# Softmax with a relative position bias: first chunk in one load, bias table spread on chip from 16 packets, first store held until the fourth load has landed

## The chip, the cores and the metric

The kernel runs on one core of one Trainium2 chip. The metric is device time in microseconds (us); the time before is the median of three runs. Besides the compute engines (TensorE is not used here), the core has 16 DMA engines, which carry every transfer between HBM (main memory) and SBUF (on-chip memory). A transfer over 128 partitions is divided among all 16.

## The reference

`logits` is 2 x 8 x 2112 x 2112 in float32, `rel_bias` is 8 x 33. A bias that depends only on the head and on the distance of row and column, clipped to 16, is added; then a softmax runs over the last axis.

```python
rel_clipped = np.clip(pos[:, None] - pos[None, :], -16, 16) + 16
bias = rel_bias[:, rel_clipped]
logits = logits + bias[None]
exp = np.exp(logits - logits.max(axis=-1, keepdims=True))
out = exp / exp.sum(axis=-1, keepdims=True)
```

285 MB are read and as many written.

## The kernel before

Each of the 128 partitions owns 264 consecutive rows of 2112 numbers; 8 partitions make one head. The rows are worked through in chunks of R = 6 rows per partition, 44 chunks in all, in four buffers X[0] to X[3] (NBUF = 4). A chunk is one transfer of 128 runs of 50688 bytes in, and one of the same size out.

Setup builds in PSUM a strip M with the bias of a partition's first row at every distance (L118 to L155 on VectorE). It begins with the bias table: ScalarE issues a load (L97) that puts the whole 8 x 33 table on each of the 128 partitions, VectorE multiplies it by a head mask (L131) and sums over the heads (L135), so that `rbS` holds the 33 numbers of the partition's own head. GpSimd supplies two index tiles for the masks.

The main loop runs over groups of four chunks (24 rows). VectorE copies a window of M to F (`strip`, L160), and then for each buffer b: `add(b)` waits for the load (`ld[b]`) and in six instructions (L166) adds the bias and takes each row's extreme; ScalarE's `exps(b)` (L175) does the exponentials and their sums; `scale(b)` on VectorE multiplies by the reciprocals (L187), and each row raises `scaled` by one.

SyncE (SP) issues all large transfers on one queue (q1 in the profile), in an order written out by hand. First come the loads of chunks 0 to 3: chunk 0 as six transfers of one row each (L88; the first five count on the semaphore `pre`, the sixth on `ld[0]`), chunks 1 to 3 as one transfer each (L78). VectorE waits for `pre` before its first `strip`. Then comes `store(0, 0)` as soon as chunk 0 is scaled, and a loop whose order is: store the next chunk (L82), wait until the store before it has landed (`st[b]`), load the chunk four further on into that buffer (L78).

```python
store(0, 0)
with nc.Fori(0, ROWS - 2 * STEP + 1, STEP, engines=[ENG.SP]) as j:
    for b in range(NBUF):
        store(j + (b + 1) * R, (b + 1) % NBUF)
        take(nc.sync, st[b], 16)
        load(j + (b + NBUF) * R, b)
```

`take` waits for a semaphore and lowers it again (L74). `store` first takes six counts of `scaled`. Each of the 16 DMA engines raises a transfer's semaphore by one when its share is done, so a wait for 16 is a wait for all of them.

Of the kernel before, what the change touches and what calls it, by code (L numbers as in the profile page):

```python
# [15 lines left out]
def kernel(  # L16
# [6 lines left out]
    nc = tc.nc  # L23
    P = 128
    B, H, S, S2 = logits.shape
    assert S == S2
    MR = 16
    W = 2 * MR + 1
    ROWS = B * H * S // P
    PB = S // ROWS  # L30
    assert ROWS * P == B * H * S and PB * ROWS == S and PB == H == 8
    R = 6
    NBUF = 4
# [9 lines left out]
    X = [io.tile([P, R * S], FP32, tag=f"X{b}", name=f"X{b}") for b in range(NBUF)]  # L43
    F = io.tile([P, FW], FP32, tag="F", name="F")
    rbS = io.tile([P, W], FP32, tag="rbS", name="rbS")
# [3 lines left out]
    ip = io.tile([P, 3, PB], I32, tag="ip", name="ip")  # L49
# [3 lines left out]
    def view(t, offset, dims):  # L53

        return bass.AP(tensor=t.tensor, offset=t.offset + offset, ap=[[list(t.ap[0])[0], P]] + dims)

    def rows(t, j, n):

        return bass.AP(tensor=t.tensor, offset=t.offset + j * S, ap=[[ROWS * S, P], [1, n * S]])

    with tc.tile_critical(no_gpsimd_drain=True):
        ld = [nc.alloc_semaphore(f"ld{b}") for b in range(NBUF)]
# [3 lines left out]
        scaled = nc.alloc_semaphore("scaled")  # L66
        inv = nc.alloc_semaphore("inv")
        rb = nc.alloc_semaphore("rb")
        pre = nc.alloc_semaphore("pre")
        idx = nc.alloc_semaphore("idx")  # L70
        dve = nc.alloc_semaphore("dve")

        def take(eng, sem, n):
            eng.wait_ge(sem, n).then_inc(sem, -n)  # L74


        def load(j, b):
            nc.sync.dma_start(out=X[b][:, :], in_=rows(logits, j, R)).then_inc(ld[b], 16)  # L78

        def store(j, b, s0=0, n=R):  # L80
            take(nc.sync, scaled, n)
            nc.sync.dma_start(  # L82
                out=rows(out, j + s0, n), in_=X[b][:, s0 * S : (s0 + n) * S]
            ).then_inc(st[b], 16)


        for r in range(R):
            nc.sync.dma_start(  # L88
                out=X[0][:, r * S : (r + 1) * S], in_=rows(logits, r, 1)
            ).then_inc(ld[0] if r == R - 1 else pre, 16)  # L90
        for n in range(1, NBUF):
            load(n * R, n)

        rbB = view(F, 0, [[1, H * W]])
        nc.scalar.dma_start(  # L97
            out=rbB,
            in_=bass.AP(tensor=rel_bias.tensor, offset=rel_bias.offset, ap=[[0, P], [1, H * W]]),
        ).then_inc(rb, 16)  # L100
        nc.gpsimd.iota(ip[:, 0], pattern=[[0, PB]], base=0, channel_multiplier=1).then_inc(idx, 1)
        nc.gpsimd.iota(ip[:, 2], pattern=[[1, PB]], base=0, channel_multiplier=0).then_inc(idx, 1)  # L102

        v = nc.vector
        done = [0]

        def then(ins):
            done[0] += 1
            ins.then_inc(dve, 1)

        def settle():
            v.wait_ge(dve, done[0])

        SC = H * W
        mask = [F[:, SC + i * PB : SC + (i + 1) * PB] for i in range(9)]
        dp, dh, eq, hm, gt, le, lt, ra, rz = mask
        v.wait_ge(idx, 2)
        then(v.tensor_scalar(out=ip[:, 1], in0=ip[:, 0], scalar1=3, scalar2=7,  # L118
                             op0=ALU.logical_shift_right, op1=ALU.bitwise_and))
# [7 lines left out]
        for m, op in ((eq, ALU.is_equal), (gt, ALU.is_gt), (le, ALU.is_le), (lt, ALU.is_lt)):  # L127
# [4 lines left out]
            out=view(F, 0, [[W, H], [1, W]]), in0=view(F, 0, [[W, H], [1, W]]),  # L132
            in1=view(F, SC + 3 * PB, [[1, H], [0, W]]), op=ALU.mult))
        settle()
        then(v.tensor_reduce(out=rbS[:, :], in_=view(F, 0, [[1, W], [W, H]]),  # L135
                             axis=mybir.AxisListType.X, op=ALU.add))
        settle()
        low, high = rbS[:, W - 1 : W], rbS[:, 0:1]
        then(v.tensor_scalar(out=ra, in0=gt, scalar1=low, scalar2=None, op0=ALU.mult))  # L139
        then(v.tensor_scalar(out=rz, in0=gt, scalar1=low, scalar2=None, op0=ALU.mult))  # L140
        then(v.tensor_tensor(  # L141
            out=view(F, 0, [[W, PB], [1, W]]), in0=view(F, SC + 2 * PB, [[1, PB], [0, W]]),
            in1=view(rbS, W - 1, [[0, PB], [-1, W]]), op=ALU.mult))
# [6 lines left out]
            out=view(M, U, [[ROWS, PB], [1, W]]), in0=view(F, 0, [[W, PB], [1, W]]),  # L150
            in1=view(F, SC + 8 * PB, [[1, PB], [0, W]]), op=ALU.add))
        then(v.tensor_copy(out=view(M, U + W, [[ROWS, PB], [1, ROWS - W]]),  # L152
                           in_=view(F, SC + 7 * PB, [[1, PB], [0, ROWS - W]])))
        then(v.tensor_copy(out=M[:, 0:U], in_=low.to_broadcast([P, U])))  # L154
# [32 lines left out]
                    v.tensor_scalar_mul(out=x, in0=x, scalar1=rec[:, r : r + 1]).then_inc(scaled, 1)  # L187

        v.sem_inc(dve, -done[0])
        take(v, pre, 16 * (R - 1))  # L190
        with nc.Fori(0, ROWS - STEP + 1, STEP, engines=[ENG.DVE]) as j:  # L191
            strip(j)
            take(v, dve, 1)
# [6 lines left out]

        store(0, 0)
        with nc.Fori(0, ROWS - 2 * STEP + 1, STEP, engines=[ENG.SP]) as j:
            for b in range(NBUF):
# [39 lines left out]
```

## Time and profile before

| What | Value |
|---|---|
| Median of 3 runs | 1331.93 us (1330.07 to 1332.26) |
| Span of the profiled execution | 1327.7 us (the page gives no other time of it) |
| VectorE (DVE) busy | 976.6 us, 74% |
| ScalarE (ACT) busy | 575.2 us, 43% |
| GpSimd (POOL) busy | 0.4 us |
| Moved by DMA | 571.11 MB, 430 GB/s over the span |

The span runs from the first to the last instruction of one execution. In the profile, a strip is the span or a window of it in 40 slices, each digit the busy share in tenths. A line of the timeline gives the start, the duration, the engine, the line of the code and the operation; "SPq" and "ACTq" are the sequencers that issue DMAs, and an issue's duration is not that of the transfer. The DMA view of a window counts the packets that start in it: a chunk's packets are of 50688 bytes, and the tiny ones are the semaphore updates at the end of each DMA engine's share. For a line that issues DMAs, another view gives the times from issue to landing.

### The profile page before, as it was taken

The numbers are of one execution on the slowest core, as the hardware profiler recorded it, in microseconds if no ns is written. First come the engines' busy times: TensorE is split into PE (matmuls) and PEld (weight loads), VectorE is DVE, ScalarE is ACT, GpSimd is POOL, SyncE is SP. The second block draws the span as 40 slices with busy tenths as digits, with TensorE's granted clock in tenths as the row PEclk, the third lists the DMA queues.
The fourth block names the chain that finished last, engine by engine and source line by source line (L and its number), as shares of the span: only waits on it lengthen the run. The fifth ranks groups of instructions, "written<-read, shape, count | busy, mean of one in ns | idle before, by whom it ended". The sixth has DMA issues, their size and how long they took to land. (4 is left out here: it accounts for less than half of the span.)

```text
span 1327.7 us, 2454 instructions
## 1 busy us (share of the span) xinstructions
DVE 976.6 (74%) x911; ACT 575.2 (43%) x539; POOL 0.4 (0%) x6
## 2 busy tenths in 40 slices
DVE  6999667777777776687778777677877776687772
ACT  2564333444444343345444333444444343335440
POOL 0000000000000000000000000000000000000000
DMA  9999999999999999999999999999999999999998
GB/s 392 431 428 437 435 420 437 435 434 425 435 437 434 428 435 434 435 429 429 438 438 432 426 438 437 437 425 437 437 437 425 435 440 437 428 432 438 437 426 359
DMA packets 13683, 571.11 MB, mean 430 GB/s; under 512 B 1521, under 2 KB 1649, under 8 KB 1649
## 3 DMA queue, kind: packets, MB, share of 16 engines
q1 hardware_dynamic: 13536, 570.96, 99.6%
q10 hardware_dynamic: 144, 0.14, 0.1%
q14 instruction: 3, 0.02, 0.0%
HBM read 285.61 MB, written 285.47 MB: 430 GB/s over the span
## 5 line engine op out<-in xcount | busy, mean ns | idle before, releaser
L166 DVE CUSTOM_DVE_ANT_0 X<-X,F 128x2112 f32<-128x2112 f32 x264 | 605.2, 2354 | 301.3 <-DVEq L74 301.3
L175 ACT ACTIVATE X<-X,nmax 128x2112 f32<-128x2112 f32 x264 | 541.7, 2052 | 539.3 <-ACTq L74 517.6
L187 DVE TENSOR_SCALAR X<-X,rec 128x2112 f32<-128x2112 f32 x264 | 332.4, 1315 | 13.2
L175 ACT ACT_TABLE_LOAD x11 | 14.1, 1283 | 183.3 <-ACTq L74 183.3
L175 ACT ACTIVATION_READ_ACCUMULATOR X<-X,nmax 128x1 f32 x264 | 49.2, 186 | 0.0
L160 DVE COPY F<-M 128x2135 f32 x11 | 26.1, 2374 | 6.3 <-DVEq L74 6.3
L166 DVE DVE_READ_ACCUMULATOR2_ANT nmax<- 128x1 f32 x264 | 21.7, 82 | 0.0
L183 DVE RECIPROCAL rec<-tot 128x3 f32<-128x3 f32 x88 | 14.9, 170 | 0.0
L131 DVE TENSOR_TENSOR F<-F 128x264 f32<-128x264 f32 x1 | 0.4, 434 | 4.7 <-DMA F<-in_rel_bias_dram 4.7
L152 DVE COPY M<-F 128x1848 f32<-128x1848 f32 x1 | 2.1, 2077 | 0.0
L118 DVE TENSOR_SCALAR ip<-ip 128x8 int32<-128x8 int32 x1 | 0.2, 173 | 1.3 <-POOL ip L102 1.3
L135 DVE TENSOR_REDUCE rbS<-F 128x33 f32<-128x264 f32 x1 | 0.6, 610 | 0.0
L149 DVE TENSOR_TENSOR M<-F 128x264 f32<-128x264 f32 x1 | 0.4, 441 | 0.0
L141 DVE TENSOR_TENSOR F<-F,rbS 128x264 f32<-128x264 f32 x1 | 0.4, 425 | 0.0
L128 DVE TENSOR_SCALAR F<-F 128x8 f32<-128x8 f32 x4 | 0.4, 166 | 0.0
L154 DVE COPY M<-rbS 128x247 f32<-128x247 f32 x1 | 0.4, 408 | 0.0
L139 DVE TENSOR_SCALAR F<-F,rbS 128x8 f32<-128x8 f32 x1 | 0.2, 231 | 0.0
L145 DVE SCALAR_TENSOR_TENSOR F<-F,rbS 128x8 f32<-128x8 f32 x1 | 0.2, 225 | 0.0
L140 DVE TENSOR_SCALAR F<-F,rbS 128x8 f32<-128x8 f32 x1 | 0.2, 222 | 0.0
L146 DVE SCALAR_TENSOR_TENSOR F<-F,rbS 128x8 f32<-128x8 f32 x1 | 0.2, 219 | 0.0
L124 DVE TENSOR_TENSOR F<-ip 128x8 f32<-128x8 int32 x1 | 0.2, 167 | 0.0
L121 DVE TENSOR_TENSOR F<-ip 128x8 f32<-128x8 int32 x1 | 0.2, 166 | 0.0
(9 smaller groups left out, 1.2 us busy)
## 6 DMA issues: line engine op xcount, KB each, us to landing
X<-in_logits_dram SPq DMA_DIRECT2D x43, 6336.0 KB, 44.6
out_dram<-X SPq DMA_DIRECT2D x43, 6336.0 KB, 52.6
X<-in_logits_dram SPq DMA_DIRECT2D x6, 1056.0 KB, 12.1
out_dram<-X SPq DMA_DIRECT2D x2, 3168.0 KB, 21.1
F<-in_rel_bias_dram ACTq DMA_DIRECT2D x1, 132.0 KB, 6.2
```

The lines of the kernel that those rows point to most:

```text
L128: then(v.tensor_scalar(out=m, in0=dp, scalar1=0.0, scalar2=None, op0=op))
L131: then(v.tensor_tensor(out=view(F, 0, [[W, H], [1, W]]), in0=view(F, 0, [[W, H], [1, W]]), in1=view(F, SC + 3 * PB, [[1, H], [0, W]]), op= ...
L135: then(v.tensor_reduce(out=rbS[:, :], in_=view(F, 0, [[1, W], [W, H]]), axis=mybir.AxisListType.X, op=ALU.add))
L141: then(v.tensor_tensor(out=view(F, 0, [[W, PB], [1, W]]), in0=view(F, SC + 2 * PB, [[1, PB], [0, W]]), in1=view(rbS, W - 1, [[0, PB], [-1, ...
L149: then(v.tensor_tensor(out=view(M, U, [[ROWS, PB], [1, W]]), in0=view(F, 0, [[W, PB], [1, W]]), in1=view(F, SC + 8 * PB, [[1, PB], [0, W]] ...
L152: then(v.tensor_copy(out=view(M, U + W, [[ROWS, PB], [1, ROWS - W]]), in_=view(F, SC + 7 * PB, [[1, PB], [0, ROWS - W]])))
L154: then(v.tensor_copy(out=M[:, 0:U], in_=low.to_broadcast([P, U])))
L160: v.tensor_copy(out=F[:, :], in_=M[:, bass.ds(ROWS - STEP - j, FW)]).then_inc(dve, 1)
L166: v.tensor_tensor_reduce(out=x, in0=x, in1=F[:, STEP - 1 - r : STEP - 1 - r + S], scale=-1.0, scalar=BIG, op0=ALU.add, op1=ALU.min, accum_ ...
L175: nc.scalar.activation(out=x, in_=x, func=EXP, scale=-1.0, bias=nmax[:, r : r + 1], accum_out=tot[:, r : r + 1],).then_inc(expd, 1)
L183: v.reciprocal(out=rec[:, r0 : r0 + HALF], in_=tot[:, r0 : r0 + HALF]).then_inc(inv, 1)
L187: v.tensor_scalar_mul(out=x, in0=x, scalar1=rec[:, r : r + 1]).then_inc(scaled, 1)
```

## The change

Three things change. Chunk 0 is loaded as one transfer like the others, and `pre` goes. The bias table is loaded on 16 partitions only, one out of every eight, in 16 packets; VectorE sets its place to zero beforehand (ScalarE's issue waits for that), and after the masking and summing it spreads the 33 numbers to the other partitions by two transposes of 32 x 32 blocks with a copy between them, and a copy to `rbS`. The fourth load counts on a new semaphore `full` instead of `ld[3]`; SP waits for all 16 counts of it before the first store, and then raises `ld[3]` by 16 itself.

```diff
-        for r in range(R):
-            nc.sync.dma_start(
-                out=X[0][:, r * S : (r + 1) * S], in_=rows(logits, r, 1)
-            ).then_inc(ld[0] if r == R - 1 else pre, 16)
-        for n in range(1, NBUF):
-            load(n * R, n)
-        rbB = view(F, 0, [[1, H * W]])
-        nc.scalar.dma_start(
-            out=rbB,
-            in_=bass.AP(tensor=rel_bias.tensor, offset=rel_bias.offset, ap=[[0, P], [1, H * W]]),
-        ).then_inc(rb, 16)
...
+        then(v.memset(F[:, 0 : H * W], 0.0))
+        nc.scalar.wait_ge(dve, 1)
+        nc.scalar.dma_start(
+            out=bass.AP(tensor=F.tensor, offset=F.offset, ap=[[PB * list(F.ap[0])[0], P // PB], [1, H * W]]),
+            in_=bass.AP(
+                tensor=rel_bias.tensor, offset=rel_bias.offset, ap=[[0, P // PB], [1, H * W]]
+            ),
+        ).then_inc(rb, 16)
+        for n in range(NBUF - 1):
+            load(n * R, n)
+        nc.sync.dma_start(
+            out=X[NBUF - 1][:, :], in_=rows(logits, (NBUF - 1) * R, R)
+        ).then_inc(full, 16)
...
+        Q = 32
+        RB, RT, RC, RW = [SC + 9 * PB + 2 * Q * i for i in range(4)]
+        then(v.memset(F[:, RB : RB + 2 * Q], 0.0))
...
-        then(v.tensor_reduce(out=rbS[:, :], in_=view(F, 0, [[1, W], [W, H]]),
+        then(v.tensor_reduce(out=F[:, RB : RB + W], in_=view(F, 0, [[1, W], [W, H]]),
                              axis=mybir.AxisListType.X, op=ALU.add))
         settle()
+        then(v.transpose(out=F[:, RT : RT + 2 * Q], in_=F[:, RB : RB + 2 * Q]))
+        settle()
+        then(v.tensor_copy(out=view(F, RC, [[Q, 2], [PB, Q // PB], [1, PB]]),
+                           in_=view(F, RT, [[Q, 2], [PB, Q // PB], [0, PB]])))
+        settle()
+        then(v.transpose(out=F[:, RW : RW + 2 * Q], in_=F[:, RC : RC + 2 * Q]))
+        settle()
+        then(v.tensor_copy(out=rbS[:, :], in_=F[:, RW : RW + W]))
+        settle()
...
         v.sem_inc(dve, -done[0])
-        take(v, pre, 16 * (R - 1))
...
+        take(nc.sync, full, 16)
+        nc.sync.sem_inc(ld[NBUF - 1], 16)
         store(0, 0)
```

More of the change, by code (lines that the diff above doesn't have):

```diff
@@ L68 @@
         rb = nc.alloc_semaphore("rb")
-        pre = nc.alloc_semaphore("pre")
         idx = nc.alloc_semaphore("idx")
         dve = nc.alloc_semaphore("dve")
+        full = nc.alloc_semaphore("full")
         def take(eng, sem, n):
@@ L84, in store @@
             ).then_inc(st[b], 16)
-        for r in range(R):
-            nc.sync.dma_start(
-                out=X[0][:, r * S : (r + 1) * S], in_=rows(logits, r, 1)
-            ).then_inc(ld[0] if r == R - 1 else pre, 16)
-        for n in range(1, NBUF):
-            load(n * R, n)
-        rbB = view(F, 0, [[1, H * W]])
-        nc.scalar.dma_start(
-            out=rbB,
-            in_=bass.AP(tensor=rel_bias.tensor, offset=rel_bias.offset, ap=[[0, P], [1, H * W]]),
-        ).then_inc(rb, 16)
-        nc.gpsimd.iota(ip[:, 0], pattern=[[0, PB]], base=0, channel_multiplier=1).then_inc(idx, 1)
-        nc.gpsimd.iota(ip[:, 2], pattern=[[1, PB]], base=0, channel_multiplier=0).then_inc(idx, 1)
         v = nc.vector
@@ L112, in settle @@
             v.wait_ge(dve, done[0])
+        then(v.memset(F[:, 0 : H * W], 0.0))
[11 more added lines that the diff above has]
+        ).then_inc(full, 16)
+        nc.gpsimd.iota(ip[:, 0], pattern=[[0, PB]], base=0, channel_multiplier=1).then_inc(idx, 1)
+        nc.gpsimd.iota(ip[:, 2], pattern=[[1, PB]], base=0, channel_multiplier=0).then_inc(idx, 1)
         SC = H * W
```

## The prediction

> **What bounds the kernel now.** I read the page first: the span, the busy shares, the strip of 40 slices, the queues.
>
> ```profile
> span 1327.7 us, 2454 instructions
> ...
> DVE 976.6 (74%) x911; ACT 575.2 (43%) x539; POOL 0.4 (0%) x6
> ...
> DMA  9999999999999999999999999999999999999998
> ...
> q1 hardware_dynamic: 13536, 570.96, 99.6%
> ```
>
> No compute engine is above 74%, while SP's queue (q1) keeps all 16 DMA engines occupied for 99.6% of the span. So only three things move the end: when the DMA engines start well, whether they ever stand idle, and whether all 16 finish together. A transfer counts as landed only when the slowest of the 16 has done its share, and the program ends with the slowest of them. The median of the runs is 1331.93, 4.2 us above the profiled span; the page gives no other time of that execution, so I work out changes against the span and carry them to the median unchanged.
>
> Second view, the timeline of SP, whose issues mark every landing it waits for: an L78 load is issued when the store of that buffer has landed on all engines.
>
> ```profile
> 0.97 3.34 SPq L88 DMA_DIRECT2D X<-in_logits_dram  x6
> 4.36 1.74 SPq L78 DMA_DIRECT2D X<-in_logits_dram  x3
> 43.07 22.23 SPq L82 DMA_DIRECT2D out_dram<-X  x2
> 81.12 0.36 SPq L78 DMA_DIRECT2D X<-in_logits_dram  x1
> 86.60 0.34 SPq L82 DMA_DIRECT2D out_dram<-X  x1
> ...
> 126.28 0.35 SPq L78 DMA_DIRECT2D X<-in_logits_dram  x1
> ...
> 638.99 0.35 SPq L78 DMA_DIRECT2D X<-in_logits_dram  x1
> ...
> 1237.05 0.35 SPq L78 DMA_DIRECT2D X<-in_logits_dram  x1
> ```
>
> From 638.99 to 1237.05 there are 20 load-and-store pairs: 598.06 / 20 = 29.90 us each. From 126.28 to 638.99 there are 17: 512.71 / 17 = 30.16 us. The same bytes cost 0.26 us more per pair in the first half, 17 x 0.256 = **4.35 us** in all, although no engine stands idle there. What is lost is lost by the slowest DMA engine alone.
>
> Third view, the DMA view of narrow windows. Every DMA engine ends its share of a transfer with one tiny packet, so the count "under 512 B" says how many of the 16 finished in that window: first the fourth load's end, then the end of a transfer near 902 us.
>
> ```profile
> DMA packets 32, 0.81 MB, mean 624 GB/s; under 512 B 16, under 2 KB 16, under 8 KB 16
> ...
> DMA packets 21, 0.61 MB, mean 1014 GB/s; under 512 B 9, under 2 KB 9, under 8 KB 9
> ...
> DMA packets 46, 1.98 MB, mean 388 GB/s; under 512 B 7, under 2 KB 7, under 8 KB 7
> ```
>
> The windows are 64.2 to 65.5, 901.9 to 902.5 and 902.5 to 907.6. At the fourth load all 16 end within 1.3 us. At 902 nine of them still end within 0.6 us of each other, and the other seven trail by up to 5.7 us. The first half is thus the time in which seven engines drop behind, in steps, until they are out of the pack's way; the nine that kept close lost nothing.
>
> **The change part by part.** *The start.* The DMA view of 0 to 8 us:
>
> ```profile
> DMA  0000000000199995276993897887995999999969
> ...
> DMA packets 345, 1.69 MB, mean 211 GB/s; under 512 B 33, under 2 KB 161, under 8 KB 161
> ...
> q1 hardware_dynamic: 200, 1.55, 58.5%
> q10 hardware_dynamic: 144, 0.14, 9.0%
> ```
>
> and the stretch 20.20 to 35.20 in the table of stretches (columns: length, DVE, ACT, POOL, clock, DMA share, GB/s):
>
> ```profile
> 20.20:35.20 15.00, 14.54 (x15) 11.54 (x12) 0.00 (x0) 1.00 1.00 433
> ```
>
> The first packets run in slice 10 of 0.2 us, at 2.0 us. By 8 us 1.69 MB are moved, which at 433 GB/s is 3.9 us of work: of 6 us, 2.1 are lost. The bias table (q10) alone holds 9.0% of 8 us = 0.72 us of every engine for 0.14 MB, because 128 small packets go between the first rows. With 16 packets, one for each engine, an eighth of that stays: 0.63 us gained for certain. The remaining 1.4 us is the mixing of both queues and the cold start; I estimate that two thirds go, 0.9. One transfer instead of six saves five sets of completions. Their price stands in the spread of landings of the six:
>
> ```profile
> L88 SPq DMA_DIRECT2D X<-in_logits_dram x6: 388/488/707, 1.0 to 3.7; - x6
> ...
> DMA to landing us min/median/max: 6.8/12.1/16.9
> ```
>
> The first lands at 1.0 + 6.8 = 7.8, the last at 3.7 + 16.9 = 20.6: 2.56 us for each of five further rows, where 1056 KB at 433 GB/s take 2.50. Six times 0.06 is 0.4 us at most. The fourth load lands earlier by 0.6 at least, 2.5 at most; I take **-2.0**, nearer to the upper end because the 0 to 8 us row shows the loss and nothing of it but the cold start is left standing.
>
> *The table on chip.* VectorE gets two memsets, two transposes and two copies, ScalarE's issue waits for the first memset, and the table now queues behind big packets.
>
> ```profile
> 7.16 0.43 DVE L131 TENSOR_TENSOR F<-F 128x264 f32<-128x264 f32 x1 [4.69 <-DMA F<-in_rel_bias_dram]
> ...
> 12.06 0.17 DVE L155 COPY M<-rbS 128x16 f32<-128x16 f32 x1
> 18.48 2.38 DVE L160 COPY F<-M 128x2135 f32 x1 [6.26 <-DVEq L74]
> 21.17 2.36 DVE L166 CUSTOM_DVE_ANT_0 X<-X,F 128x2112 f32<-128x2112 f32 x1 [0.31 <-DVEq L74]
> ```
>
> The table's chain ends at 12.2 and stands before a wait of 6.26 us. No transpose is in the trace; between the 0.17 us of a small operation and the 0.43 of a 264-wide one, the four serial steps cost 0.7 to 1.7 us, the memset before the issue 0.4. Even with 2 us of queueing the chain ends near 16. The strip copy (L160) no longer waits for five of the six rows, so it runs inside that idle time and chunk 0 begins when it lands. That makes the first stores *ready* about 2.7 us earlier (21.17 - 18.48), which nobody uses: SP does not issue then. Zero on the end. If this cover failed by some microseconds, the next one holds: chunk 0 would be ready near 40, and the barrier opens after 63.
>
> *The barrier.* SP now waits on `full` before store 0. Queued behind it on SP are stores 0 and 1 (43.07 and near 65 in the trace), then the wait for store 0, the fifth load and everything else. VectorE takes chunk 3 only after chunk 2, near 84 (86.60 is store 2's issue), so getting `ld[3]` from SP costs nothing. What it costs is that the queue is empty at its end.
>
> ```profile
> L78 SPq DMA_DIRECT2D X<-in_logits_dram x43: 349/349/664, 4.4 to 1237.1; - x43
> L78 SPq FUSED_REGOPS  x40: 46/46/46, 81.0 to 1236.9; - x40
> ...
> DMA to landing us min/median/max: 30.0/44.6/60.3
> ```
>
> The fourth load is the third of the L78 issues that end at 6.10; one takes 0.35 to 0.66, so it was issued near 5.6, and it lands 60.3 later, at 65.9; the slowest engine's completion packet was out by 65.5, so the signal takes 0.4. Two more SP instructions near 46 ns, with the wake-up, are 0.2. From SP's issue to its first packets it was 0.97 to between 2.0 and 2.3: 1.0 to 1.3. The restart of all 16 spreads over 0 to 0.7. Before, the slowest engine went straight from load to store; now it stands still for 1.6 to 2.6 us; I take **+2.2**, since the whole start-up of the trace is nearest in kind. The Trainium skill, page "DMA: Bandwidth & Descriptors", section "Latency and other measured facts", puts a hardware queue's first byte at about 600 ns; by that the restart would be some 0.6 us shorter and the time as much lower, but this trace has 1.0 or more for it.
>
> *What the barrier returns.* All engines begin store 0 within the spread of one restart instead of 1.3 us, and the start has fewer packets to pull them apart. The nine that stay within 0.6 us hold 29.90 us a pair for 600 us, so a pack that close loses nothing. If all 16 are in it, the 4.35 us of the first half stay away; I leave 0.5 for single stragglers: **-3.9**.
>
> Sum: 1331.93 - 2.0 + 2.2 - 3.9 = **1328.2**.
>
> **The rivals.** *The pack breaks up again.* The seven could be pushed out by what happens when engines change from load to store together, whatever they started with. For it: at 64.2 to 65.5 they were only 1.3 us apart, and that did not hold. Against it: nine held. Then nothing returns: 1331.93 - 2.0 + 2.2 = 1332.1, no measurable change. The same page, section "Rules for kernel authors", advises to issue a DMA early and wait late. By it the barrier is a loss without return, and it is this rival's time that would come out.
>
> *The pack never settles.* Slower: 29.90 us was reached in the trace only once seven engines were clear of the others. If a tight start of all 16 keeps them colliding at each changeover, the 0.256 us a pair lasts for all 40 pairs that begin with an L78 load behind a store, 10.2 us instead of 4.35: 1332.1 + 5.9 = 1338.0. It decides if more than about nine further pairs stay at 30.16 (9 x 0.256 = 2.3, and 0.2 from above). For it: the period took 500 us to settle. Against it: an engine only ever lost time until it was out of the way, which a fresh start does not prevent. Between these ends, its middle is 1335.
>
> *The start gains little.* If the loss of 0 to 8 us is the cold start and not the table, only 0.6 comes, and the restart is cold too: 1331.93 - 0.6 + 2.6 - 3.9 = 1330.0, about no change; if the pack breaks up as well, 1333.9.
>
> **How the numbers follow.** A measurement of this kernel tells about 0.2% (2.7 us) from no change. Forecast 0.52, pack breaks up 0.14, never settles 0.24, start gains little 0.10: the evidence of the nine for the forecast, the 500 us of settling for the second, and both starts seen only once for the last. The forecast's own range is 1326.7 (1331.93 - 2.5 + 1.6 - 4.35) to 1329.4, the line below which it counts as faster. Faster is the forecast's 0.52; same is the first and the last rival, 0.24, as both of the last one's times are within 0.2%; slower is the never-settling pack, 0.24. The range reaches from 1326.3, a little under the forecast's lower end since the runs shown scatter by 1 us about their middle, to 1335, leaving out the upper half of the never-settling case, 0.12, and some 0.05 below.
>
> **What would show it.** The fourth load lands near 64 instead of 65.9. Store 0 is issued then, the DMA strip shows one gap of about 2 us behind it, and the fifth load is issued near 81. From there pairs take 29.90 us at once; 30.1 or more between 126 and 640 says the pack broke up, and the same beyond 640 that it does not settle. At the end the 16 completions lie within 1 us instead of 5.7. I am wrong if the gap is over 3 us, or if the end trails as before.

## The result, and the profile after

| | Before | After |
|---|---|---|
| Median | 1330.91 us (1328.45 to 1333.08, 8 runs) | 1334.61 us (1332.70 to 1335.86, 8 runs) |
| Ratio after / before | | 1.0026 (1.0018 to 1.0035) |
| Span of the profiled execution | 1327.7 us | 1332.3 us (time 1334.32) |

The changed kernel is slower by 0.26%, about 3.5 us. The prediction had 1328.2 and "faster"; 1334.6 lies inside its range, on the other side of no change.

The page of after, beside the lines of before shown in the prediction:

```profile
span 1332.3 us, 2456 instructions
...
DVE 977.8 (73%) x917; ACT 575.2 (43%) x539; POOL 0.4 (0%) x6
...
q1 hardware_dynamic: 12816, 570.96, 99.4%
q10 hardware_dynamic: 32, 0.02, 0.0%
```

Compute is unchanged, and the DMA queue still bounds everything. q10, the bias table, has shrunk from 144 packets in the first 8 us to 32 records in all. The window 0 to 8 us of after:

```profile
DMA  0000000009999000000000999500000699950000
DMA packets 64, 2.45 MB, mean 306 GB/s; under 512 B 0, under 2 KB 16, under 8 KB 16
```

Only large packets go, in three clean rounds. 2.45 MB are under way by 8 us instead of 1.69; 0.76 MB at 433 GB/s are 1.8 us.

The timeline of SP in after:

```profile
2.35 0.60 SPq L108 DMA_DIRECT2D X<-in_logits_dram  x1
64.27 1.12 SPq L82 DMA_DIRECT2D out_dram<-X  x2
80.88 0.36 SPq L78 DMA_DIRECT2D X<-in_logits_dram  x1
84.22 0.34 SPq L82 DMA_DIRECT2D out_dram<-X  x1
...
128.24 0.35 SPq L78 DMA_DIRECT2D X<-in_logits_dram  x1
...
642.25 0.35 SPq L78 DMA_DIRECT2D X<-in_logits_dram  x1
...
1241.63 0.35 SPq L78 DMA_DIRECT2D X<-in_logits_dram  x1
```

The fourth load (L108) has landed on all engines just before 64.27, when the first store is issued; before it landed at 65.9. The load that follows store 0 is issued at 80.88 instead of 81.12: gain of the start and cost of the wait have nearly cancelled. But the load issued at 128.24 was issued at 126.28 before. So 2.2 us are lost between 81 and 128, where both kernels have nothing but loads and stores queued without a gap. From 128.24 to 642.25 there are 17 pairs of 30.24 us (before 30.16), from there to 1241.63 twenty of 29.97 (before 29.90).

Where those 2.2 us go is seen in the DMA view in narrow windows. Of after, in this order: 62 to 66, 80 to 80.4, 84 to 90, 92 to 98 and 108 to 114 us. A slice counts the packets that start in it, so a strip shows when the 16 engines take their next packet.

```profile
DMA  0000000000000000000000000000000990000000
DMA packets 32, 0.81 MB, mean 203 GB/s; under 512 B 16, under 2 KB 16, under 8 KB 16
...
DMA packets 32, 0.81 MB, mean 2028 GB/s; under 512 B 16, under 2 KB 16, under 8 KB 16
...
DMA  9000000000079000000000009900000000007900
...
DMA  8000000099000800000000009999900000000099
...
DMA  0000000999000000000000000999990700000999
```

The same two last windows, 92 to 98 and 108 to 114, of before:

```profile
DMA  0099997900700079799970700009999790070007
...
DMA  7009000099979070077099997970009009997907
```

- Strip 1: no packet of a chunk starts until 65.1, then all 16 engines start store 0 within 0.2 us. That is the barrier's gap.
- The row of 80 to 80.4: all 16 tiny completion packets of store 0 lie in 0.4 us. The change does level the engines.
- Strip 3 is the regular run of levelled engines: one burst each 1.87 us.
- Strip 4: after the burst at 93.2 the next comes not 1.87 but 2.4 to 3.1 us later. This is the last packet of store 1 on 15 of the 16 engines, ahead of a load (the last engine, at 94.0, took only 0.1 us more).
- Strip 5: the same between 109.1 and 111.8 to 112.7, the last packets of the fifth load, ahead of a store.
- The strips of before have starts spread over the whole window, and no such hole.

I call this an all-engine stall. By the trace's packet records, from which all landings and stalls below are worked out, a packet of 50688 bytes takes 1.872 us; the packets at the end of store 1 took 0.8 us more in the mean of 16 engines, those at the end of the fifth load 1.1 more. In before the same two places cost 0.06 and 0.10. All stalls below are such sums over the packets around a change between load and store, good to about 0.1 us.

With the landing of the first engine (which lost least) and of the last (which sets the end), in us:

| Transfer | Before: first / last | After: first / last | Change: first / last |
|---|---|---|---|
| Chunk 0 | 19.77 / 20.58 | 17.97 / 18.60 | -1.8 / -2.0 |
| Fourth load | 64.73 / 65.94 | 62.93 / 64.04 | -1.8 / -1.9 |
| Store 0 | 79.68 / 80.89 | 80.48 / 80.66 | +0.8 / -0.2 |
| Store 1 | 95.00 / 95.83 | 96.08 / 96.66 | +1.1 / +0.8 |
| Fifth load | 109.66 / 111.10 | 112.13 / 112.99 | +2.5 / +1.9 |
| Last store | 1320.94 / 1326.56 | 1323.54 / 1331.15 | +2.6 / +4.6 |

The first engine's column is the sum of the change: -1.8 from the start, +2.6 from the gap, +1.7 from two stalls, and nothing in the 1200 us after. The last engine's adds 2.0, because the levelled engines spread again, from 0.9 us at the fifth load to 7.6 at the end, further than before (5.6). The DMA view of 1323.8 to 1331.3 of after:

```profile
DMA packets 39, 0.79 MB, mean 105 GB/s; under 512 B 8, under 2 KB 8, under 8 KB 8
```

Half of the engines' final packets still come in those 7.5 us, where the prediction wanted 16 within 1 us. All experiments but one (the changed order of stores and loads) end with a spread between 6.4 and 9.1, so the 5.6 of before was small: of the 4.6 us between the two profiled executions, about 1 is chance, which fits the 3.5 of the medians.

### The profile page after: what moved, and what is told of

Read it like the earlier page. It is cut to its first block, busy times and chain, and to the rows that moved or that the text cites. A ratio compares the mean times of both kernels' runs of the same rounds, so it can differ in the third digit from the quotient of the medians.

```text
span 1332.3 us, 2456 instructions
## 1 busy us (share of the span) xinstructions
DVE 977.8 (73%) x917; ACT 575.2 (43%) x539; POOL 0.4 (0%) x6
```

## The experiments

"First" and "last" are the first and last engine's end, before having 1320.9 and 1326.6. Ratios are against before, run on the same chip.

**The two halves of the change, alone.** Only the start (after, without the wait):

```diff
-        for n in range(NBUF - 1):
+        for n in range(NBUF):
             load(n * R, n)
-        nc.sync.dma_start(
-            out=X[NBUF - 1][:, :], in_=rows(logits, (NBUF - 1) * R, R)
-        ).then_inc(full, 16)
...
-        take(nc.sync, full, 16)
-        nc.sync.sem_inc(ld[NBUF - 1], 16)
         store(0, 0)
```

> The new start alone (chunk 0 as one transfer, table in 16 packets), no barrier. Theory U (unison): what costs time in the changed kernel is the barrier, which makes all 16 DMA engines change between storing and loading at the same moment, whereupon all of them stall. Then this run keeps the 2.0 us of the start and nothing else: fourth load landed near 64.0, no empty queue, the last packets before the change to the fifth load and before the third store no longer than in the kernel before, time 2 us under before (0.15%). Theory S (start): the even start itself makes the pack too tight, and the barrier costs only its idle time. Then the stalls of 0.8 to 1.1 us near 93 and 109 us show here too, and the time is no better than before, up to 2 us worse.

Measured: 1330.66, ratio 1.0002 (0.9994 to 1.0011). Chunk 0 lands as early as in after (17.97 / 18.63), but the fourth load at 63.87 / 65.56 instead of 62.93 / 64.04. Its DMA view of 59 to 65:

```profile
DMA  9977007000099999009000000000009999700000
```

The burst at 60.7 to 61.4 is followed by the next only at 63.5 to 64.2: an all-engine stall of 1.0 us in the mean, at the first change from load to store, without any gap in the queue. First 1319.98, last 1326.91. The start gains its 1.8 us and pays 1 back at once; the rest goes in the spread, 6.9.

Only the wait (before, fourth load on `full`):

```diff
-        for n in range(1, NBUF):
+        for n in range(1, NBUF - 1):
             load(n * R, n)
+        nc.sync.dma_start(
+            out=X[NBUF - 1][:, :], in_=rows(logits, (NBUF - 1) * R, R)
+        ).then_inc(full, 16)
...
+        take(nc.sync, full, 16)
+        nc.sync.sem_inc(ld[NBUF - 1], 16)
         store(0, 0)
```

> The kernel before with the barrier alone. Theory U: an empty queue of about 2.2 us after the fourth load, then both stalls of all engines, about 1.9 us together at the slowest, and as much trailing after that as in the changed kernel: 4 to 7 us above before (0.3 to 0.5%). Theory S: the idle time alone, 2.2 us above before, no stall of all engines near 95 and 111 us.

Measured: 1335.58, ratio 1.0039 (1.0026 to 1.0052); first 1325.63, last 1332.94. DMA view of 64 to 68 and 94 to 100:

```profile
DMA  0000000000000000000000000000009990000000
...
DMA  0000000099000800000000009999900000000799
```

The gap and the stalls (0.8 and 1.1 in the mean) are those of after, almost slice for slice. So the wait, with what follows it, is the loss, and returns nothing; the start is what softens it.

**Pushing half of the engines back behind the wait.** After, with a small store to 8 partitions ahead of store 0:

```diff
+        SW = 6912
+        scr = nc.dram_tensor("scr", (8, SW), FP32, kind="Internal").ap()
...
-        store(0, 0)
+        take(nc.sync, scaled, R)
+        nc.sync.dma_start(out=scr, in_=X[0][0:8, 0:SW]).then_inc(extra, 16)
+        nc.sync.dma_start(out=rows(out, 0, R), in_=X[0][:, :]).then_inc(st[0], 16)
```

> The changed kernel with an extra transfer of 8 partitions by 27648 bytes ahead of the first store, which holds 8 of the 16 DMA engines back by 1.0 us after the barrier; its output goes to a scratch tensor. Theory U: two halves 1.0 us apart no longer change in unison, so the stalls near 93 and 109 us fall from 0.85 and 1.06 us (mean of the 16) to under 0.4, and the fifth load lands no later than in the changed kernel (113.0) although half the engines carry 1.0 us more; time equal to the changed kernel or up to 1 us better. If the stalls have another cause (the place after the restart, the compute beside them), they stay and the time is 1.0 us above the changed kernel.

Measured: 1335.60, ratio 1.0040 (1.0025 to 1.0055); first 1323.86, last 1331.96. DMA view of 64.5 to 70.5:

```profile
DMA  0009999970000000000090000000000999099000
```

The eight small packets (slices 3 to 8, with the other engines' chunk packets) held their engines 4.0 to 4.8 us, not the 1.0 that their 27648 bytes should take at the rate of the large ones. The two halves were thus 3.8 to 4.3 us apart. Two stalls came all the same (0.6 and 0.9 in the mean), the first on the eight engines in front and four of those behind. Then the spread stayed near 4.8 from 117 to 300 us, with pairs of 29.90 at once, until one engine drifted to 8.1. So far apart, the engines hardly spread further for a time; the push costs what the spreading would.

**A wait in mid-run.** Before, with the same wait at the load of chunk 27:

```diff
+        MID = 5 * STEP
+        steady(0, MID)
+        for b in range(NBUF):
+            store(MID + (b + 1) * R, (b + 1) % NBUF)
+            take(nc.sync, st[b], 16)
+            if b < NBUF - 1:
+                load(MID + (b + NBUF) * R, b)
+        nc.sync.dma_start(
+            out=X[NBUF - 1][:, :], in_=rows(logits, MID + (2 * NBUF - 1) * R, R)
+        ).then_inc(full, 16)
+        take(nc.sync, full, 16)
+        nc.sync.sem_inc(ld[NBUF - 1], 16)
+        steady(MID + STEP, ROWS - 2 * STEP + 1)
```

> The kernel before with such a barrier in mid-run instead (SP waits for the load of chunk 27, near 820 us, before the next store), when the engines have long been settled. Theory U: idle 2.2 us, then at the next two changes of direction all engines stall (about 1.9 us together), and trailing grows again from near nothing: 5 to 8 us above before (0.4 to 0.6%). If the stalls belong to the first transfers of the run and not to the engines being level: only the idle time, 2.2 us above before, and the trailing at the end is smaller than before.

Measured: 1340.35, ratio 1.0072 (1.0058 to 1.0087); first 1332.75, last 1339.11. DMA view of 804 to 808 and 834 to 840:

```profile
DMA  0000000000000000000000000009990000000000
...
DMA  9907000000099909000000000000099997000000
```

Here the engines had been 7.9 us apart, so the first ones stood idle for 9 us, and the time is 10 us over before, more than either theory said. After it, the same two stalls (0.9 and 0.9), none at the third change, and the spread grows again from 0.7 to 6.4. The two stalls thus follow a restart from an empty queue wherever it is, not only the beginning of the kernel; the spread is the state that levelled engines return to.

**Apart from the start.** Only the start (as in the first experiment), with extra loads to 8 partitions ahead of chunk 0; with `range(1)`, and with `range(2)`:

```diff
+        for i in range(1):
+            nc.sync.dma_start(
+                out=X[2 + i][0:8, :],
+                in_=bass.AP(tensor=logits.tensor, offset=logits.offset, ap=[[ROWS * S, 8], [1, R * S]]),
+            ).then_inc(extra, 16)
+        for n in range(2):
+            load(n * R, n)
+        take(nc.sync, extra, 16)
+        for n in range(2, NBUF):
             load(n * R, n)
```

> The new start without the barrier, and ahead of it one extra load of 8 partitions by 50688 bytes, which keeps 8 of the 16 DMA engines back by one packet (about 1.9 us) from the first microsecond on; what it loads is overwritten. Theory U, sharpened (engines that change direction while close together stall and drop back; two groups some 3.5 us apart did not for 500 us in the run with the held half): a distance of 1.9 us is in between, so the stall of all engines near 62 us becomes one of half of them (under 0.6 us as the mean of the 16), and trailing still grows, but from a start of 2 us; time between 2 us under and equal to the kernel before. If trailing has nothing to do with the distance of the engines, it grows by its 4 to 6 us on top of the 1.9: 2 to 3 us above before.

> The same with two extra loads: 8 engines are two packets (3.7 us) late from the start. Theory U: this is the distance at which nothing was lost for 500 us; after the first changes of direction every pair takes 29.9 us, the end spreads by 4 to 5 us instead of 5.6 to 7.7, and the time is 1 to 4 us under before (0.1 to 0.3%). If trailing does not depend on the distance: the 3.7 us come on top, 3 to 5 us above before.

Measured with one: 1335.28, ratio 1.0032 (1.0020 to 1.0044); first 1324.68, last 1332.31. Chunk 0 landed at 23.20 / 24.86, the halves 1.35 to 1.65 apart. No stall at the first change. But between 200 and 204 us all engines stalled (0.6 in the mean) without any gap in the queue, and the spread grew from there to 7.6. With two: 1340.79, ratio 1.0075 (1.0062 to 1.0089); first 1329.81, last 1337.65. DMA view of 2 to 16 with two:

```profile
DMA  9000009900000009999900000990000000000969
```

A packet to one of these 8 partitions took 5.4 to 6.7 us in the first extra load and 7.5, four times 1.87, in the second; the first two chunk packets of the other eight engines, beside them, took 6.2 to 6.6 as well. Chunk 0 landed at 28.95 / 32.51, 11 us late on the first engine. From there the first engine lost nothing: halves about 3 us apart, no stall, 1300.86 us from chunk 0's landing to the end on the first engine, where the start alone takes 1302.01. Fifteen engines end within 4.3 us; one drifted to 7.8, by 0.06 us a transfer from about 430 us on. So far apart, and without a restart, the other engines neither stalled nor spread, but setting them apart cost far more than the 1.2 us that it saved.

**Fewer changes of direction.** Before, with two stores and then two loads in turn:

```diff
-            for b in range(NBUF):
-                store(j + (b + 1) * R, (b + 1) % NBUF)
-                take(nc.sync, st[b], 16)
-                load(j + (b + NBUF) * R, b)
+            for b in range(0, NBUF, 2):
+                for i in (1, 2):
+                    store(j + (b + i) * R, (b + i) % NBUF)
+                for i in (0, 1):
+                    take(nc.sync, st[b + i], 16)
+                    load(j + (b + i + NBUF) * R, b + i)
```

> The kernel before with SP's loop in pairs: two stores, then two loads, so that the DMA engines change direction half as often for the same bytes. Theory U: what is lost at each change comes half as often, so that the trailing takes twice as long to grow; at the end it is 3 to 4.5 us instead of 5.6, and the time 1 to 3 us under before (0.1 to 0.2%), provided no wait of SP empties the queue. If the losses go by time or bytes and not by changes of direction: no difference.

Measured: 1333.83, ratio 1.0026 (1.0016 to 1.0036); first 1326.03, last 1329.96. With half the changes the spread grows more slowly (3.2 at 409 us, before 4.7; 4.8 at 648, before 5.7), yet reaches 6.1. From 118 to 545 us the packets lost 0.8 us in the mean of 16 engines, half of before's 1.6, as they should if the changes of direction drive it. The packet records of before say where: from 118 to 1250 us, 82 packets took over 0.1 us more than usual, and 79 of them are an engine's last packet of a load, ahead of a store; none is the last of a store. The first engine lost 5 us: all engines stalled near 795 and 1217 us (0.7 each in the mean, no gap in the queue), and 2.1 went near the end, where the first part of the last store was late and the queue ran empty. That gap also levelled the engines from 6.1 to 3.9. Not a better order.

**Smaller pushes.** As in the push behind the wait, but with the small store read from every fourth partition (0, 4 to 28) instead of 8 neighbours: half a chunk packet (`SW = 6336`), and a whole one (`SW = 12672`).

```diff
-        SW = 6912
+        SW = 6336
...
-        nc.sync.dma_start(out=scr, in_=X[0][0:8, 0:SW]).then_inc(extra, 16)
+        nc.sync.dma_start(out=scr, in_=X[0][0:32:4, 0:SW]).then_inc(extra, 16)
```

> The changed kernel with an extra transfer after the barrier as in the run with the held half, but over partitions 0, 4, ... 28, and 25344 bytes each: 8 of the 16 DMA engines are held back by half of a big packet (0.93 us, if such a spread lets it run at the usual rate; over partitions 0 to 7 a packet took four times as long). Theory P (phase): all 16 engines stall at a change of direction when their packets begin within about 0.6 us of each other, counted within the packet time of 1.87 us. Then the two stalls near 93 and 109 us fall under 0.3 us in the mean, the leaders reach the end about 1.9 us earlier than in the changed kernel, and the time is 1 to 2 us under it. Theory R (restart): the first two changes after any restart stall whatever the spread. Then both stalls stay at 0.7 to 1.1 us and the time is 0.9 us over the changed kernel.

> The same with 50688 bytes: half of the engines are held back by one whole packet (1.87 us), so that they change direction 1.87 us after the others, but all 16 begin their packets together. Theory P: both stalls stay (0.7 us or more), time 1.9 us over the changed kernel. Theory U (only engines that change direction at the same time disturb each other): both stalls fall to about half. Theory R: both stay, as by P; the run with half a packet tells these two apart.

Measured with half: 1334.83, ratio 1.0035 (1.0022 to 1.0049); first 1324.55, last 1331.65. The packets took 0.96 us, as their size says, and the halves were 0.55 apart. Stalls 0.8 and 1.4; DMA view of 93 to 99:

```profile
DMA  9000700099009000070000000099099090000099
```

There are two groups, with bursts at 94.2 and 94.8, and their next at 96.9 and 97.4: both take 2.6 to 2.7 us instead of 1.87. That a stall needs all 16 packets to end at once is refuted. With a whole packet: 1336.82, ratio 1.0052 (1.0037 to 1.0068); first 1325.99, last 1333.29; halves 1.5 apart, stalls 1.1 and 1.0. After a restart, the next two changes of direction stall whether the engines are 0.2, 1.5 or 4 us apart. In this last run all 16 also stalled later, near 261 us (0.8 in the mean), without any gap in the queue.

Only the start, with such small loads ahead of chunk 0: half a packet (`[6336]`), and one and a half (`[12672, 6336]`):

```diff
+        for i, w in enumerate([6336]):
+            nc.sync.dma_start(
+                out=X[3 - i][0:32:4, 0:w],
+                in_=bass.AP(tensor=logits.tensor, offset=logits.offset, ap=[[4 * ROWS * S, 8], [1, w]]),
+            ).then_inc(extra, 16)
```

> The new start without the barrier and with an extra load over partitions 0, 4, ... 28 of 25344 bytes ahead of everything, so that 8 engines run half a packet (0.93 us) late from the start. Theory P: the stall of 1.0 us of all engines that the new start alone had near 61 us disappears; the leaders end about 1 us earlier than with the new start alone (near 1319), trailing grows to 6 to 8 us as in all runs with a close pack; time equal to the kernel before or up to 1.5 us under it. Rival: the stall stays, and the time is 1 us over the new start alone.

> The same with 50688 and 25344 bytes: 8 engines run one and a half packets (2.8 us) late. By the run with two early extra loads, where a distance of 3.0 us lost nothing for the whole run apart from one engine that drifts by 0.04 us a transfer, no stalls and no trailing are expected: leaders near 1319, the end 3.5 to 4.5 us behind them, or 7 if the drifting engine is among the late ones; time 1 to 4 us under the kernel before in the first case, equal to it in the second. If trailing depends on something else, 6 to 8 us come on top of the 2.8: 2 us or more over the kernel before.

Measured with half: 1332.37, ratio 1.0017 (1.0008 to 1.0026); first 1321.42, last 1330.55. The push was swallowed by the cold start: all engines within 0.60 at chunk 0, stall 1.0 at the first change. With one and a half: 1334.50, ratio 1.0036 (1.0022 to 1.0049); first 1322.52, last 1330.54; halves 1.1 to 1.5 apart, stall 0.5, spread to 8.0.

**Which part of the start, and is waiting itself the harm?** Before, with chunk 0 as one transfer only; before, with the 16-packet table only (the table's part of the change, without its loads); and before, with the first store held until the *third* load has landed, when the fourth still fills the queue:

```diff
-        for r in range(R):
-            nc.sync.dma_start(
-                out=X[0][:, r * S : (r + 1) * S], in_=rows(logits, r, 1)
-            ).then_inc(ld[0] if r == R - 1 else pre, 16)
-        for n in range(1, NBUF):
+        for n in range(NBUF):
             load(n * R, n)
```

> The kernel before with chunk 0 as one transfer, the table still in 128 packets, no barrier. The new start alone landed the fourth load 1.8 us earlier but stalled all engines by 1.0 us at their first change of direction. If the single transfer brings that stall, it shows here near 63 us (1.0 us in the mean of the 16), and the time is equal to the kernel before or up to 1 us over it, since the table still costs what it did; if it does not, the stall is under 0.2 us and the time is equal to before or up to 0.5 us under it.

> The kernel before with the table in 16 packets spread on chip, chunk 0 still as six transfers, no barrier. If the few packets of the table bring the stall of the new start, it shows here near 61 us (1.0 us in the mean) and the time equals that of the kernel before; if not, the start's gain of 1.5 to 1.8 us stays and the time is 1.5 us under before (0.1%), the trailing being as in before.

```diff
-        for n in range(1, NBUF):
-            load(n * R, n)
+        load(R, 1)
+        nc.sync.dma_start(out=X[2][:, :], in_=rows(logits, 2 * R, R)).then_inc(full, 16)
+        load(3 * R, 3)
...
+        take(nc.sync, full, 16)
+        nc.sync.sem_inc(ld[2], 16)
         store(0, 0)
```

> The kernel before with the first store held until the third load has landed on all engines, not the fourth, so that the fourth load is still queued and the queue does not run empty. If the harm comes from the empty queue and the restart at one moment: no idle time, no stall of all engines at the two changes near 95 and 111 us, time equal to the kernel before within 1 us. If holding the store back does harm by itself (the stores bunched, SP late): stalls or a later fifth load as with the full barrier, 2 us or more over before.

Measured: one transfer 1330.59, ratio 1.0002 (0.9993 to 1.0011), chunk 0 at 19.24 / 19.99. Table 1331.60, ratio 1.0015 (1.0006 to 1.0024), chunk 0 at 18.30 / 18.74. Third load 1329.78, ratio 0.9996 (0.9987 to 1.0006). Their DMA views of 60 to 66, first one transfer:

```profile
DMA  7999070070007999770070007799907007000799
```

then the table:

```profile
DMA  7000009999009000000007799990000070999997
```

then the third load:

```profile
DMA  7009999900709000999990707700999990070900
```

Only the table's strip has a hole, from 61.8 to 63.2: the fourth load's last packets took 0.65 more in the mean. The six row loads cost 0.6 us and the 128 small packets 1.8; but small packets had also kept the engines 0.8 us apart at chunk 0. Without them it is 0.45, and the first change stalls. Over the kernels that change from load to store without a gap, those with 0.45 to 0.65 us at chunk 0 (table, start alone, half packet) stall there by 0.65 to 1.0, and those with 0.75 to 1.4 (before, one transfer, third load, the wait in mid-run, pairs) do not. But of two with halves set apart, one at 1.1 to 1.5 us stalled by 0.5 and one at 1.35 to 1.65 not at all, so the spread is hardly the whole condition.

The third load is the control for the wait: SP waits on a landing there too, but the queue holds another load meanwhile, and nothing is lost. The early stalls came only where the queue had run empty or the start was tight. Later in a run all engines stalled now and then without either, near 200, 261, 795 and 1217 us in three of the kernels; these runs do not show why.

None of these kernels beats before; the first and the last equal it.

## Why the prediction was wrong, step by step

- **The start, -2.0: right.** Chunk 0 came 2.0 earlier and the fourth load 1.9. The split was not: I put 0.6 for certain on the table, 0.4 at most on the six transfers and 0.9 on mixing. Alone, the table brings 1.8 and the one transfer 0.6 (both together 2.0, so they overlap): most of the gain hangs on the table's small packets. How much of that is their own time and how much their mixing with the rows was not separated.
- **The table on chip, 0 on the end: right.** The timeline of VectorE in after:

```profile
9.30 0.43 DVE L135 TENSOR_TENSOR F<-F 128x264 f32<-128x264 f32 x1 [6.84 <-DMA F<-in_rel_bias_dram]
...
10.41 0.24 DVE L142 STREAM_TRANSPOSE F<-F 128x64 f32<-128x64 f32 x1
...
11.20 0.18 DVE L149 COPY rbS<-F 128x33 f32<-128x33 f32 x1
...
15.86 2.38 DVE L173 COPY F<-M 128x2135 f32 x1 [0.48 <-DVEq L202]
18.79 2.36 DVE L179 CUSTOM_DVE_ANT_0 X<-X,F 128x2112 f32<-128x2112 f32 x1 [0.55 <-DVEq L74]
```

  The table arrives 2.1 us later, as allowed for. The four added steps run from 10.41 to 11.38, 0.97 us (bounds 0.7 to 1.7). The strip copy is done at 18.24, before chunk 0's landing at 18.6, and the first add starts 2.4 us earlier than before; nobody uses it, as said.
- **The barrier, +2.2: within its bounds, but priced on one engine.** From the fourth load's landing at 64.04 it is 0.2 us to SP's issue at 64.27, and 0.8 from there to the first packet at 65.1, less than the 1.0 that the start of the kernel takes. From the fourth load to store 0 the last engine's change goes from -1.9 to -0.2, so the wait cost it 1.7, half a microsecond under the 2.2; the first engine's goes from -1.8 to +0.8, 2.6, because it now waits for the last one as well. The prediction priced the slowest engine only, since it alone sets the end. As all 16 spread again from the level, the first engine's loss is the one that lasts.
- **What the barrier returns, -3.9: wrong, and this is the step that failed.** "A pack that close loses nothing" was read from nine engines that had settled after 900 us, and put on 16 engines just levelled. They lost in two ways. At once: 1.7 us on the first engine and 2.1 on the last in the two changes behind the restart, seen in all six kernels that restart from an empty queue (after, the wait alone, both smaller pushes and the larger one, and the wait in mid-run). Later: the pack broke up again, by 2.0 more than in before. Counted on the last engine, as the prediction counts, -1.9 of the start, +1.7 of the wait and +4.8 make the +4.6 between the two profiled executions: the term put at -3.9 measured +4.8, about 1 of it chance.
- **The rivals.** "The pack breaks up again" names the mechanism, with 1332.1; the stalls make it 1332.1 + 1.7 = 1333.8, and 1334.6 was measured. The prediction quoted the Trainium skill, "DMA: Bandwidth & Descriptors", "Rules for kernel authors", on issuing early and waiting late: by that rule, as the prediction reads it (the page gives it for hiding a DMA behind compute), the wait is a loss without return, and the runs agree, the wait alone costing 0.39%. The control shows its limit: a wait with another transfer still queued costs nothing. "Never settles" did not come: 29.97 beyond 642. Nor did "the start gains little", although its 1333.9 with a broken pack comes near: the start gave its 1.9. That 1334.6 lies inside the range is luck, since the range reached up to 1335 only for the rival that did not come.
- **A number under all terms.** The prediction took 4.2 us between span and time, from the median. The runs with both show 2.0 (1334.32 - 1332.3) and 1.8 (1329.81 - 1328.0, the start alone). The profiled execution of before was thus a good one, near 1329.6, with the smallest end spread of all kernels that keep its order of transfers; its 5.7 us of trailing were taken as a loss to be removed, when they are the kernel's usual state or better.

Of the causes, these are shown: the idle gap and the two stalls come with an empty queue (the wait alone, the wait in mid-run, the control), and the earlier start comes mostly from the table's packets. Open is why the engines stall there together: neither their spread nor the step of their packets decides it, since halves 1.5 and 4 us apart stalled after a restart while halves 1.4 us apart without one did not at their first change. A restart brings the stalls, but it is not the only thing that does, as the later ones without a gap show. Also open is why the spread stops growing between 5.6 and 9.

## What to carry to other kernels

On a kernel bound by its DMA queue, do not let the queue run empty to put engines in order: here the order did not last, and all engines paid for the restart. If a wait is needed, keep one more transfer queued behind it, which cost nothing here. Before treating unequal finishing as a loss to be removed, look for it in several executions and try what a levelled run does; and price a wait on the first engine as well as on the slowest.

## What the runs showed of the hardware

- A transfer over 8 neighbouring partitions ran at about a quarter of the rate: 4.0 to 4.8 us for 27648 bytes stored and 5.4 to 7.5 us for 50688 loaded, where a store over partitions 0, 4 to 28 took 0.96 us for 25344. As a load it also slowed the chunk packets of the other engines beside it, to 5.7 to 6.6 us; as a store it did not (1.9).
- After a restart from an empty queue, the engines stalled at the next two changes between load and store, by 0.6 to 1.4 us in the mean of 16, and not at the third, in six kernels of six. Such stalls also came, seldom, without a gap in the queue.
- In steady alternation, engines fall behind at the end of a load that a store follows: 79 of 82 slow packets in before, none at the end of a store.
- 128 small packets mixed into a start cost 1.8 us more than 16 of them.
- In two kernels one single engine drifted back by about 0.06 us a transfer, from some 400 to 600 us on to the end.
